# DeltaNet phase of a hybrid block: the order of each head's matmuls given explicitly instead of by a list scheduler

## The chip, the cores and the metric

One core of a Trainium2 chip (trn2). The metric is the device time of one execution in microseconds (us), the median over the runs shown. Engines: PE is the matrix engine (TensorE), PEld its weight loads, DVE the vector engine, ACT the scalar engine, POOL the general engine (GpSimd), SP the engine that issues most DMAs. Each engine works through its own list of instructions in the order of that list; an instruction that is not ready holds up what stands behind it on that engine.

## The reference, cut to what matters

The kernel computes one block of a network: 1024 tokens and 256 context tokens of width 1024; two attention branches over one input projection, gated and merged, then a squared-relu MLP. The change is in the second branch, DeltaNet, with 8 heads of width 128:

```python
def prep(p):
    qkv = silu(depthwise_conv_centred(concatenate([p[3], p[4], p[5]], -1), conv_w))
    q, k, v = split(qkv, 3, -1)
    q = l2_normalize(hd(q)) * DN_HEAD_DIM ** -0.5
    k = l2_normalize(hd(k))
...
def gated_delta_rule(q, k, v, g, beta, s0):          # once forward, once backward
    a_mat = where(strict, einsum('bhnid,bhnjd->bhnij', kb, kc) * decay, 0.0)
    t_mat = triangular_solve(eye + a_mat, eye)        # inverse within a chunk
    ...
    def step(state, xs):
        v_new = u_i - einsum('bhid,bhde->bhie', w_i, state)
        o_i = einsum('bhid,bhde->bhie', q_i, state) + einsum('bhij,bhje->bhie', qk_i, v_new)
        state = state * g_i + einsum('bhid,bhie->bhde', k_i, v_new)
        return state, o_i
...
out_x = rms_norm(ox_f + flip(ox_b), norm_g) * silu(zx)
```

## The kernel before, in words

The DeltaNet phase (`dn_phase`) lies at about 187 to 1340 us of the span. Ahead of it are the modulation of the inputs and small projections; behind it are the attention heads, the merge and the MLP, which the change does not touch but for one call.

A head goes through these parts. **Projections** (`dn_proj` for v, k and q, `dn_gate` for z): each is 48 matmuls of 128x512, two groups of 512 tokens by 8 slices by 3 products (the operands are split in a high and a low part, lines 164 to 166). k, q and v then go through a convolution of 7 taps on DVE (L440; the first tap on ACT, then 6 DVE instructions for each of the two token groups) and Silu on ACT. Further projections that the attention branch needs later are "fills"; they depend on nothing in the heads. **Preparation** (`dn_prep`): sums of squares of k and q for the norms, decay matrices by matmuls (L467, L470), k by k and q by k products (L520, L528), out of which `cm` (the matrix to be inverted, one 128x128 block for each of 10 chunks and both directions) and `pm` come. The 32x32 blocks on the diagonal of `cm` are written to DRAM and read back so that 80 blocks lie in partitions (104 of them with a gap), then inverted by 48 instructions in a row on DVE: a copy (L540), 15 pairs L565 and L566, 4 pairs L573 and L575, 4 pairs L579 and L582, a copy (L545). The inverses go to DRAM again as `xd` and `yd` (L550, L551). **Doubling** (`dn_double`): 7 loads for each direction bring them back into `cm` and `tt` (L596, L599), then 100 matmuls of 32x32 and 40 of 64x64 (both directions together) put the 128x128 inverse together. These are fp32, and an fp32 matmul counts as two passes on PE in the profile. **Tokens** (`dn_pre`): transposes of v and k. **Recurrence** (`dn_chain`): 10 steps for each of two directions; in a step a state matmul (L676), `xs` on DVE (L678), a `cm` matmul (L680), `ws` on ACT (L683), a k matmul (L688), the new state on DVE (L691, L693), and beside it the output (L698 to L707). Then the norm of the output `oacc` on DVE and ACT (to L719), and 8 transposes with the gate (L723, L725).

While the recurrence of head h runs, head h+1 is prepared and v of h+1, k and q of h+2, z of h+1 and fills are projected. In `dn_phase` these are written one after the other; a list scheduler with ranks (0 first: recurrence, doubling, evictions; then preparation and inverse, rank 1; convolution, rank 2) decides where each instruction stands in its engine's list.

The tiles `z32`, `z64`, `tt`, `oacc` have one buffer, `cm` and `pm` four, that is two heads.

Of the kernel before, what the change touches and what calls it, by code (L numbers as in the profile page):

```python
# [35 lines left out]
ORD = 'vkqffz'  # L36
GAP = 8
SPLIT = 508
W1 = (2, 4)
# [14 lines left out]
class K:  # L54
    def __init__(self, tc, ins, out, ctx):
        self.tc, self.nc, self.i, self.out, self.ctx = tc, tc.nc, ins, out, ctx
        self.ranks = None
        self.weng = tc.nc.vector

# [94 lines left out]
    def gemm_cols(self, w, u, toks, evac, cs=slice(0, P), pool=None):  # L154

        nc = self.nc
        rh, rl = u
        for t0, n in toks:
            ps = (pool or self.pg).tile([P, 512], F32, name="pc" if pool else "pg")
            o = ps[:, :n]  # L160
            for k in range(KT):
                hi, lo = w[k][0][:, cs], w[k][1][:, cs]
                a, b = rh[:, k, t0:t0 + n], rl[:, k, t0:t0 + n]
                nc.tensor.matmul(o, lhsT=hi, rhs=a, start=k == 0, stop=False)  # L164
                nc.tensor.matmul(o, lhsT=hi, rhs=b, start=False, stop=False)  # L165
                nc.tensor.matmul(o, lhsT=lo, rhs=a, start=False, stop=k == KT - 1)  # L166
            with self.rank(R_E):
                evac(o, t0, n)
# [246 lines left out]
    def dn_proj(self, h, nm, res):  # L415
# [13 lines left out]
        self.gemm_cols(w, (self.uh, self.ul), TOKS_X, lambda ps, t0, n: nc.scalar.copy(out=raw[:, XO + t0:XO + t0 + n], in_=ps))  # L429
# [13 lines left out]
        res[nm] = acc  # L443

# [5 lines left out]
    def dn_gate(self, h, res):  # L450
        nc, i = self.nc, self.i
        u = (self.uh, self.ul)
        w = self.weight(i["w_in"][0, :, O_DNZ + h * P:O_DNZ + (h + 1) * P])
        sz = self.dw.tile([P, SEQ], F32, name="sz", bufs=1)
        self.gemm_cols(w, u, TOKS_X, lambda ps, t0, n: nc.scalar.activation(out=sz[:, t0:t0 + n], in_=ps, func=AF.Silu))
        res["z"] = sz

    def dn_decay(self, d, h, c0, n, masked):
# [4 lines left out]
        for part, (g, nm) in enumerate(((self.gh[d], "ugh"), (self.gl[d], "ugl"))):  # L463
# [3 lines left out]
            nc.tensor.matmul(pd[:, :n], lhsT=self.r_gt if d == 0 else self.r_lt, rhs=ug[:, :n], start=part == 0,  # L467
                             stop=part == 1 and not masked)
        if masked:
            nc.tensor.matmul(pd[:, :n], lhsT=self.r_id, rhs=self.r_neg[d].unsqueeze(1).to_broadcast((P, n, P)), start=False, stop=True)  # L470
# [4 lines left out]
    def dn_prep(self, h, r):  # L475
# [4 lines left out]
        groups = ((0, 4), (4, 4), (8, 2))  # L480
        ss = ds.tile([P, NT + NX], F32, name="ss")
        ssk, ssq = ss[:, 0:NT], ss[:, NT:]
        for c0, n in groups:
            pt = self.pt.tile([P, 4, P], F32, name="pt")
            for c in range(n):
                nc.tensor.transpose(out=pt[:, c, :], in_=self.ck(kT, c0 + c), identity=self.ident)
            for c in range(n):
                sq = ds.tile([P, P], F32, name="sq", bufs=1)
                nc.scalar.activation(out=sq, in_=pt[:, c], func=AF.Square, accum_out=ssk[:, c0 + c:c0 + c + 1])
        for c0, n in ((0, 4), (4, 4)):  # L490
            pt = self.pt.tile([P, 4, P], F32, name="pt")
            for c in range(n):
                nc.tensor.transpose(out=pt[:, c, :], in_=ch(qT, c0 + c), identity=self.ident)
            for c in range(n):
                sq = ds.tile([P, P], F32, name="sq", bufs=1)
                nc.scalar.activation(out=sq, in_=pt[:, c], func=AF.Square, accum_out=ssq[:, c0 + c:c0 + c + 1])
        nc.vector.tensor_scalar(out=ss, in0=ss, scalar1=RMS_EPS, scalar2=None, op0=ALU.add)
# [18 lines left out]
        for c0, n in ((0, NC0), (NC0, 4), (NC0 + 4, 4)):  # L516
            dec = [self.dn_decay(d, h, c0, n, c0 > 0) for d in range(2)]
            pk = self.pt.tile([P, 4, P], F32, name="pt")
            for c in range(n):
                nc.tensor.matmul(pk[:, c], lhsT=self.ck(kT, c0 + c), rhs=self.ck(kT, c0 + c), start=True, stop=True)  # L520
            for c in range(n):
                for d in range(2):
                    nc.vector.scalar_tensor_tensor(out=cm[d][:, c0 + c], in0=pk[:, c], scalar=nb2[d][:, c0 + c:c0 + c + 1],
                                                   in1=dec[d][:, c], op0=ALU.mult, op1=ALU.mult)
            if c0:
                pk = self.pt.tile([P, 4, P], F32, name="pt")
                for c in range(n):
                    nc.tensor.matmul(pk[:, c], lhsT=self.ck(kT, c0 + c), rhs=ch(qT, c0 + c - NC0), start=True, stop=True)  # L528
                for d in range(2):
                    nc.vector.tensor_tensor(out=pm[d][:, c0 - NC0:c0 - NC0 + n], in0=pk, in1=dec[d], op=ALU.mult)  # L530

# [52 lines left out]
    def dn_double(self, h, r):  # L584
# [3 lines left out]
        tt = []  # L588
        for d in range(2):
            t = dw.tile([P, NT, 64], F32, name="tt", bufs=BK[0])  # L590
            for b, (lo, hi) in (((0, (32, 128)), (1, (64, 128)), (2, (96, 128))) if d else ((1, (0, 32)), (2, (0, 64)), (3, (0, 96)))):
                nc.gpsimd.memset(cm[d][32 * b:32 * b + 32, :, lo:hi], 0.0)
            nc.gpsimd.memset(t[96:128, :, 0:32] if d else t[0:32, :, 32:64], 0.0)
            for b in range(4):
                s = slice(32 * b, 32 * b + 32)
                nc.sync.dma_start(out=cm[d][s, :, s], in_=(yd if d else xd)[d, b].rearrange("c j i -> j c i"))  # L596
                if b != (0 if d else 3):
                    o = 32 * (b % 2)
                    nc.sync.dma_start(out=t[s, :, o:o + 32], in_=(xd if d else yd)[d, b].rearrange("c j i -> j c i"))  # L599
            tt.append(t)  # L600

        for d in range(2):
            c_, t_ = cm[d], tt[d]
            pairs = ((3, 2), (1, 0)) if d else ((0, 1), (2, 3))
            sl = lambda b: slice(32 * b, 32 * b + 32)
            co = lambda b: slice(32 * (b % 2), 32 * (b % 2) + 32)
            pz = self.po.tile([P, NT, 32], F32, name="po")
            z = dw.tile([P, NT, 32], F32, name="z32", bufs=1)
            for a, b in pairs:
                for c in range(NT):  # L610
                    nc.tensor.matmul(pz[sl(b), c], lhsT=c_[sl(a), c, sl(b)], rhs=t_[sl(a), c, co(a)], start=True, stop=True)
                nc.vector.tensor_copy(out=z[sl(b)], in_=pz[sl(b)])
            py = self.po.tile([P, NT, 32], F32, name="po")
            a, b = pairs[0]
            for c in range(NT):
                nc.tensor.matmul(py[sl(b), c], lhsT=c_[sl(b), c, sl(b)], rhs=z[sl(b), c], start=True, stop=True)
            nc.scalar.copy(out=t_[sl(b), :, co(a)], in_=py[sl(b)])
            px = self.po.tile([P, NT, 32], F32, name="po")
            for a, b in pairs:
                for c in range(NT):  # L620
                    nc.tensor.matmul(px[sl(a), c], lhsT=z[sl(b), c], rhs=c_[sl(b), c, sl(b)], start=True, stop=True)
                nc.scalar.copy(out=c_[sl(a), :, sl(b)], in_=px[sl(a)])
            A, B = (slice(64, 128), slice(0, 64)) if d else (slice(0, 64), slice(64, 128))
            z6 = dw.tile([P, NT, 64], F32, name="z64", bufs=1)
            for q in range(2):
                pz = self.po.tile([P, 5, 64], F32, name="po")
                for c in range(5):
                    nc.tensor.matmul(pz[B, c], lhsT=c_[A, 5 * q + c, B], rhs=t_[A, 5 * q + c, :], start=True, stop=True)
                nc.vector.tensor_copy(out=z6[B, 5 * q:5 * q + 5], in_=pz[B])
            for q in range(2):  # L630
                px = self.po.tile([P, 5, 64], F32, name="po")
                for c in range(5):
                    nc.tensor.matmul(px[A, c], lhsT=z6[B, 5 * q + c], rhs=c_[B, 5 * q + c, B], start=True, stop=True)
                nc.scalar.copy(out=c_[A, 5 * q:5 * q + 5, B], in_=px[A])

    def dn_pre(self, h, r):

        nc, dw, ds = self.nc, self.dw, self.ds
        kT, vT = r["k"], r["v"]
        ch = lambda a, c: a[:, c * P:(c + 1) * P]  # L640

        vtok = dw.tile([P, NT, P], F32, name="vtok", bufs=1)
        for c0, n in ((0, 4), (4, 4), (8, 2)):
            pt = self.pt.tile([P, 4, P], F32, name="pt")
            for c in range(n):
                nc.tensor.transpose(out=pt[:, c, :], in_=self.ck(vT, c0 + c), identity=self.ident)
            for c in range(n):
                nc.scalar.activation(out=vtok[:, c0 + c], in_=pt[:, c], func=AF.Copy, scale=r["sk"][:, c0 + c:c0 + c + 1])
        ktok = dw.tile([P, NT, P], F32, name="ktok", bufs=1)
        for c0, n in ((0, 4), (4, 4), (8, 2)):  # L650
            pt = self.pt.tile([P, 4, P], F32, name="pt")
            for c in range(n):
                nc.tensor.transpose(out=pt[:, c, :], in_=self.ck(kT, c0 + c), identity=self.ident)
# [944 lines left out]
```

## Time and profile before

| | |
|---|---|
| median of 3 runs (3024.41, 3024.48, 3035.09) | 3024.48 us |
| the profiled execution's own time | 3038.64 us |
| its span in the profile | 3036.9 us |
| PE busy | 2828.2 us, 93% |
| DVE busy | 2008.3 us, 66% |
| ACT busy | 1333.1 us, 44% |
| POOL busy | 656.6 us, 22% |

How to read the views: a line of the timeline has the start and length of an instruction or a run of alike ones in us, the engine, the line of the kernel, the operation, output<-inputs (tile names), the tile, the type, the count, and in brackets the idle time just before with what ended it. Matmuls are pipelined, so that the step from one start to the next is what one costs, not the length shown. A line of the windows view has start:end and length, then busy us (instructions) of PE, PEld, DVE, ACT and POOL, the granted clock of PE as a share of 2.4 GHz, the DMA share and GB/s.

### The profile page before, as it was taken

How to read it: one execution, taken by the hardware profiler on the slowest of the kernel's cores; microseconds unless marked ns; L12 is line 12 of the kernel's file. 1: busy time of each engine (PE TensorE's matmuls, PEld its weight loads, DVE VectorE, ACT ScalarE, POOL GpSimd, SP SyncE). 2: the span in 40 equal slices, each digit the busy share in tenths (PEclk: the TensorE clock that was granted, in tenths of full speed). 3: DMA queues.
4: the chain of work that ended last, by engine and by line, in shares of the span. 5: the costliest groups of instructions: out<-in, count | busy, mean ns of one | idle time of the engine just before them, and what ended most of it. 6: DMA issues, size and time to landing. Idle time of an engine off the chain costs nothing. (4 is left out here: it accounts for less than half of the span.)

```text
span 3036.9 us, 44469 instructions
## 1 busy us (share of the span) xinstructions
PE 2828.2 (93%) x15928; PEld 2273.6 (75%) x15928; DVE 2008.3 (66%) x3675; ACT 1333.1 (44%) x3269; POOL 656.6 (22%) x756
## 2 busy tenths in 40 slices
PE   7998989899898999989999999899999999989998
PEld 4886768677686777868887778677777677768887
DVE  4768497794967767247777778664486776544435
ACT  4655244444443544326655556564465422322210
POOL 1234223532423241021111110101001643100000
PEclk9999799998998999789999999999999999999999
DMA  7631211211212122173433332416564544453321
GB/s 253 190 110 43 52 48 34 67 53 41 70 33 66 34 63 67 37 186 81 105 93 93 91 88 66 91 39 198 158 220 131 164 143 120 137 194 104 104 63 63
DMA packets 340973, 303.09 MB, mean 100 GB/s; under 512 B 87892, under 2 KB 287700, under 8 KB 339728
## 3 DMA queue, kind: packets, MB, share of 16 engines
q1 hardware_dynamic: 318864, 252.14, 28.5%
q10 hardware_dynamic: 18304, 37.41, 4.8%
q0 software_dynamic: 3584, 10.71, 1.0%
q8 instruction: 125, 2.05, 0.3%
q14 instruction: 96, 0.79, 0.1%
HBM read 212.08 MB, written 66.06 MB: 92 GB/s over the span
## 5 line engine op out<-in xcount | busy, mean ns | idle before, releaser
L150 POOL TENSOR_TENSOR wlo<-wraw,whi 128x256 fp32r<-128x256 f32 x312 | 320.7, 1033 | 1219.5 <-ACT whi L149 987.3
L164 PE MATMUL pg<-uh,whi 128*128 128x512 f32 x1152 | 481.7, 418 | 6.6 <-ACT whi L149 3.2
L166 PE MATMUL pg<-uh,wlo 128*128 128x512 f32 x1152 | 481.3, 418 | 6.1 <-POOL wlo L150 5.8
L165 PE MATMUL pg<-ul,whi 128*128 128x512 f32 x1152 | 481.4, 418 | 0.0
L149 ACT CAST whi<-wraw 128x256 fp32r<-128x256 f32 (+1 forms) x568 | 241.0, 430 | 322.9 <-PE pg L165 102.9
L166 PEld LDWEIGHTS pg<-uh,wlo 128*128 128x128 f32 x1152 | 224.6, 195 | 49.9 <-POOL wlo L150 11.1
L164 PEld LDWEIGHTS pg<-uh,whi 128*128 128x128 f32 x1152 | 224.9, 195 | 47.0 <-ACT whi L149 4.8
L165 PEld LDWEIGHTS pg<-ul,whi 128*128 128x128 f32 x1152 | 224.8, 195 | 39.6
L1370 PE MATMUL pa<-B,A 128*128 128x512 f32 x768 | 220.6, 395 | 13.6 <-ACT B L1318 5.0
L1370 PE MATMUL pg<-B,A 128*128 128x512 f32 x768 | 219.5, 393 | 0.0
L150 DVE TENSOR_TENSOR wlo<-wraw,whi 128x256 fp32r<-128x256 f32 (+1 forms) x256 | 136.6, 542 | 120.8 <-ACT whi L149 119.1
L888 DVE TENSOR_REDUCE mp<-sx 128x1 f32<-128x1024 f32 x128 | 155.7, 1218 | 49.8 <-PE sx L878 49.4
L1370 PEld LDWEIGHTS pa<-B,A 128*128 128x128 f32 x768 | 145.9, 190 | 46.9 <-ACT B L1318 5.4
L1370 PEld LDWEIGHTS pg<-B,A 128*128 128x128 f32 x768 | 146.2, 190 | 30.7
L893 ACT ACTIVATE p<-sx,mx 128x1024 f32<-128x1024 f32 x128 | 143.2, 1118 | 53.2 <-DVE mx L889 41.9
L916 PEld LDWEIGHTS pat<-V,aT 128*128 128x128 f32 x1280 | 151.0, 193 | 14.6 <-ACT aT L914 12.1
L916 PE MATMUL pat<-V,aT 128*128 128x128 f32 x1280 | 158.8, 279 | 0.0
L913 PE MATMUL pat<-ident,p 128*128 128x128 f32 x640 | 119.6, 285 | 8.0 <-ACT oh L917 5.0
L1386 DVE TENSOR_TENSOR acc<-pa,acc 128x512 f32<-128x512 f32 x32 | 22.1, 690 | 157.0 <-PE pa L1370 157.0
L1318 ACT CAST A<-araw 128x1024 fp32r<-128x1024 f32 x32 | 33.6, 1052 | 209.7 <-PE pg L1370 171.8
L913 PEld LDWEIGHTS pat<-ident,p 128*128 128x128 f32 x640 | 74.6, 142 | 56.2 <-ACT aT L914 21.3
L877 PE MATMUL sx<-K,Q 128*128 128x512 f32 x256 | 109.5, 428 | 2.9 <-DMA wraw<-in_w_in_dram 2.0
(457 smaller groups left out, 6701.8 us busy)
## 6 DMA issues: line engine op xcount, KB each, us to landing
wraw<-in_w_in_dram SPq DMA_DIRECT2D x288, 128.0 KB
wraw<-in_w_in_dram SPq DMA_DIRECT2D x64, 256.0 KB
uraw<-in_w_mlp_dram SPq DMA_DIRECT2D x32, 512.0 KB
braw<-in_w_mlp_dram SPq DMA_DIRECT2D x32, 512.0 KB
araw<-ff_d SPq DMA_DIRECT2D x32, 512.0 KB
ff_d<-ue SPq DMA_DIRECT2D x52, 256.0 KB
adraw<-in_w_ada_dram SPq DMA_DIRECT2D x32, 320.0 KB
wa<-in_w_ada_dram SPq DMA_DIRECT2D x8, 1024.0 KB
```

The source lines that it names most:

```text
L149: nc.scalar.copy(out=hi, in_=raw)
L150: self.weng.tensor_tensor(out=lo, in0=raw, in1=hi.bitcast(F32), op=ALU.subtract)
L164: nc.tensor.matmul(o, lhsT=hi, rhs=a, start=k == 0, stop=False)
L165: nc.tensor.matmul(o, lhsT=hi, rhs=b, start=False, stop=False)
L166: nc.tensor.matmul(o, lhsT=lo, rhs=a, start=False, stop=k == KT - 1)
L877: nc.tensor.matmul(ps, lhsT=Q[m][:, qs], rhs=Kh[m][:, ks], start=True, stop=False)
L888: nc.vector.tensor_reduce(out=mp[:, m, 0:1], in_=px[m], axis=AX.X, op=ALU.max)
L893: nc.scalar.activation(out=p[:, CTX:], in_=px[m], func=AF.Exp, bias=mx[:, m:m + 1], accum_out=sp[:, 0, m:m + 1])
L913: nc.tensor.transpose(out=pt[:, c], in_=a[:, (c0 + c) * P:(c0 + c + 1) * P], identity=self.ident)
L916: nc.tensor.matmul(po, lhsT=aT[:, c], rhs=r["v"][:, c], start=c == 0, stop=c == NT - 1)
L1318: nc.scalar.copy(out=z[:, 0], in_=x)
L1370: mm = lambda x, y, **kw: nc.tensor.matmul(ps[c], lhsT=a[:, x, k], rhs=bt[:, y, s], **kw)
```

## The change: the matmuls of a head in a given order

Each matmul and transpose of the phase now goes through `mm` or `tp`, and from the first recurrence on each depends on the one before it, which waits for nothing but fixes PE's order (`pe`, `pinned`). Projections become generators that give one matmul at a time. Between the three parts of a recurrence step ("a" the state matmuls of both directions, "b" the `cm` matmuls, "c" the k and output matmuls) stand 5, 6 and 4 projection matmuls; the next head's preparation comes piece by piece behind parts a and c. Behind the recurrence come the output's transposes after 36 projection matmuls, the tokens from 44 on in five pieces 8 apart, and the next head's doubling in 8 pieces, 8 projection matmuls apart, with 60 left before the first. Both directions are doubled before the next recurrence starts (before, the second direction's doubling stood among the recurrence of the first), and the loads for the second direction are issued after the third piece of the first. z of head h is projected in the round of head h instead of h-1, the number of fills in a round is a table, and the last fills of the attention branch's values move behind the loop. The sums of squares are made in another way: one Square on ACT over the whole tile, then 18 matmuls with 2 columns against ones, where there were 18 transposes and 18 Squares with an accumulator.

```diff
+NFILL = (2, 2, 2, 1, 2, 1, 3, 3)
+GAPS = (5, 6, 4)
+FIN, PRE, PRS, DBL, DBS = 36, 44, 8, 60, 8
...
+    def pe(self, x):
+
+        if self.pinned is not None:
+            if self.pinned:
+                self.tc.add_manual_dep(x.ins, self.pinned, mybir.DependencyInfo(
+                    mybir.DependencyClass.NoSync, mybir.DependencyReason.DATA), reason="given order")
+            self.pinned = x.ins.name
+        return x
+
+    def mm(self, out, lhsT, rhs, start=True, stop=True):
+        return self.pe(self.nc.tensor.matmul(out, lhsT=lhsT, rhs=rhs, start=start, stop=stop))
...
+        if nm != "v":
+            with self.rank(R_PREP):
+                nc.scalar.activation(out=raw[:, 0:acc.shape[1]], in_=acc, func=AF.Square)
+            res["s" + nm] = raw
+
+    def dn_sums(self, nm, r):
...
+        for c in range(n):
+            self.mm(ps[:, c], raw[:, c * P:(c + 1) * P] if nm == "q" else self.ck(raw, c), self.ones)
...
+        self.pinned = ""
         for h in range(H):
...
+            big = self.round(h, proj)
+            left = NBIG[h]
...
+            prep = ranked(self.dn_prep(h + 1, R[h + 1]), R_PREP) if h + 1 < H else iter(())
+            for step, part in self.dn_chain(h, R[h]):
+                take(GAPS["abc".index(part)])
+                if part != "b":
+                    next(prep, 0)
+            all_of(prep)
+
+            rest = [(FIN, lambda: self.dn_finish(h, R[h]))]
             if h + 1 < H:
...
+                pre = ranked(self.dn_pre(h + 1, R[h + 1]), R_PREP)
+                rest += [(PRE + PRS * j, lambda: next(pre)) for j in range(5)]
+                rest += [(max(left - DBL + DBS * j, FIN + 1), x) for j, x in enumerate(self.dn_double(h + 1, R[h + 1]))]
...
+    def round(self, h, proj):
+
+        yield from proj(h + 1, "v")
+        yield from proj(h, "z")
+        n = NFILL[h]
+        yield from self.fill(n // 2)
+        yield from proj(h + 2, "k", "q")
+        yield from self.fill(n - n // 2)
+        if h == H - 1:
+            yield from self.fill_head()
```

Two places show what the lists become. On PE before, in the middle of a round (the doubling of head 2, first direction), the first doubling matmuls (`po<-tt,cm`, fp32) stand among preparation products of the next head (`pt<-kT`, `pt<-qT,kT`) and few projections (`pg`):

```order
L611 MATMUL po<-tt,cm 32x32 x10
L520 MATMUL pt<-kT 128x128 x2
L528 MATMUL pt<-qT,kT 128x128
L616 MATMUL po<-z_5944,cm 32x32 x10
L528 MATMUL pt<-qT,kT 128x128 x3
L621 MATMUL po<-cm,z_5944 32x32 x10
L164 MATMUL pg<-uh,whi 128x512
L165 MATMUL pg<-ul,whi 128x512
L166 MATMUL pg<-uh,wlo 128x512
L611 MATMUL po<-tt,cm 32x32 x10
```

On PE now, in the same doubling (every matmul has the line of the helper, L74):

```order
L74 MATMUL pg<-uh,wlo 128x512
L74 MATMUL po<-tt,cm 32x32 x20
L74 MATMUL pg<-uh,whi 128x512
L74 MATMUL pg<-ul,whi 128x512
L74 MATMUL pg<-uh,wlo 128x512
L74 MATMUL pg<-uh,whi 128x512
L74 MATMUL pg<-ul,whi 128x512
L74 MATMUL pg<-uh,wlo 128x512
L74 MATMUL pg<-uh,whi 128x512
L74 MATMUL pg<-ul,whi 128x512
L74 MATMUL po<-z_5383,cm 32x32 x10
L74 MATMUL po<-cm,z_5383 32x32 x20
```

Moved is what stands between two pieces of the doubling: eight projection matmuls, counted out, with no preparation beside them.

On DVE before, the copy that begins an inverse (L540, that of head 3, in the round of head 2) stands among the recurrence's early steps (`xs` L678, the states L693) and the convolution of v:

```order
L693 SCALAR_TENSOR_TENSOR S_6198<-S_6164,edec,pc_6188 128x128
L440 SCALAR_TENSOR_TENSOR vT<-cvraw,taps,vT 128x516
L678 SCALAR_TENSOR_TENSOR xs_6224<-pc_6222,necg,vtok 128x128
L440 SCALAR_TENSOR_TENSOR vT<-cvraw,taps,vT 128x516
L693 SCALAR_TENSOR_TENSOR S_6152<-S_6132,edec,pc_6144 128x128
L440 SCALAR_TENSOR_TENSOR vT<-cvraw,taps,vT 128x516
L678 SCALAR_TENSOR_TENSOR xs_6173<-pc_6171,necg,vtok 128x128
L540 COPY slL<-slY 40x1024
L565 TENSOR_TENSOR slY<-slX,slL 104x2
L707 TENSOR_TENSOR oacc<-po,oacc 128x128
L693 SCALAR_TENSOR_TENSOR S_6181<-S_6152,edec,pc_6171 128x128
L566 TENSOR_REDUCE slX<-slY 104x2
```

On DVE now, at the same inverse, the copy has the line L570, and the last two `xs` of the recurrence (L729, its tenth step) stand ahead of it:

```order
L767 TENSOR_TENSOR oacc<-po,oacc 128x128
L766 SCALAR_TENSOR_TENSOR oacc<-po,edec,oacc 128x128
L767 TENSOR_TENSOR oacc<-po,oacc 128x128
L729 SCALAR_TENSOR_TENSOR xs_6423<-pc_6420,necg,vk_5301 128x128
L729 SCALAR_TENSOR_TENSOR xs_6426<-pc_6421,necg,vk_5301 128x128
L766 SCALAR_TENSOR_TENSOR oacc<-po,edec,oacc 128x128
L570 COPY slL<-slY 40x1024
L767 TENSOR_TENSOR oacc<-po,oacc 128x128
L766 SCALAR_TENSOR_TENSOR oacc<-po,edec,oacc 128x128
L595 TENSOR_TENSOR slY<-slX,slL 104x2
L767 TENSOR_TENSOR oacc<-po,oacc 128x128
L596 TENSOR_REDUCE slX<-slY 104x2
```

The inverse has moved from among the first steps of the recurrence to behind its last. From this copy to the inverse's last copy (L545 before, L575 now) DVE's list holds 48 instructions of the inverse in both kernels; the others between were 13 of the convolution, 47 of the recurrence and 17 of the norm and output, and are now 18, 3 and 17.

## Rows read from the trace of the kernel before

**Rows 1.** Windows view: the heads' stretch of the phase, then two short ones.

```profile
343.20:1231.00 887.80, 816.93 (x5595) 661.38 (x5594) 644.75 (x1423) 392.18 (x1117) 288.08 (x334) 0.92 0.20 52
676.00:684.00 8.00, 8.00 (x35) 6.31 (x34) 7.44 (x11) 1.99 (x7) 5.21 (x2) 1.00 0.16 57
687.00:697.00 10.00, 10.00 (x79) 8.27 (x80) 0.48 (x1) 5.80 (x20) 2.37 (x7) 0.50 0.42 116
```

**Rows 2.** Timeline of PE: first matmuls of three recurrences (heads 0, 2, 7).

```profile
343.18 0.80 PE L680 MATMUL pc<-vtok,cm 128*128 128x128 f32 x2
...
590.05 0.49 PE L680 MATMUL pc<-vtok,cm 128*128 128x128 f32 x2
...
1230.95 0.79 PE L680 MATMUL pc<-vtok,cm 128*128 128x128 f32 x2
```

**Rows 3.** Waits of PE, 343 to 1231 us: total us, times, longest.

```profile
PE po L723 <- DVE oacc L719: 24.5, 6, 11.0
```

**Rows 4.** DVE by line, 343.2 to 1231 us: busy us, mean ns; idle.

```profile
L440 DVE SCALAR_TENSOR_TENSOR kT<-cvraw,taps,kT 128x772 f32<-128x772 f32 (+1 forms) x72 | 64.0, 888 | 0.0
L440 DVE SCALAR_TENSOR_TENSOR qT<-cvraw,taps,qT 128x516 f32<-128x516 f32 (+1 forms) x72 | 54.4, 767 | 0.4
L565 DVE TENSOR_TENSOR slY<-slX,slL 104x2 f32<-104x2 f32 (+14 forms) x105 | 52.6, 501 | 0.8
...
L579 DVE TENSOR_TENSOR slY<-slL,slX 104x256 f32<-104x256 f32 (+3 forms) x28 | 39.5, 1412 | 0.3
...
L573 DVE TENSOR_TENSOR slY<-slX,slL 104x1024 f32<-104x1024 f32 (+3 forms) x28 | 37.1, 1325 | 0.1
...
L566 DVE TENSOR_REDUCE slX<-slY 104x2 f32<-104x2 f32 (+14 forms) x105 | 33.5, 319 | 0.7
...
L575 DVE TENSOR_REDUCE slL<-slY 104x64 f32<-104x1024 f32 (+3 forms) x28 | 22.7, 810 | 0.1
...
L725 DVE SCALAR_TENSOR_TENSOR sz<-po,dng,sz 128x512 f32<-128x512 f32 x14 | 9.8, 738 | 0.0
...
L719 DVE TENSOR_TENSOR oacc<-oacc,soy 128x1024 f32<-128x1024 f32 x7 | 8.5, 1212 | 0.0
```

**Rows 5.** Timeline of DVE: an inverse's first and last copy, another's last.

```profile
615.94 1.11 DVE L540 COPY slL<-slY 40x1024 f32<-40x1024 f32 x1
...
674.60 1.10 DVE L545 COPY slY<-slX 104x1024 f32<-104x1024 f32 x1
...
1205.11 1.43 DVE L545 COPY slY<-slX 104x1024 f32<-104x1024 f32 x1
```

**Rows 6.** Timeline of PE: the doublings' first matmuls after those two last copies.

```profile
686.95 1.24 PE L611 MATMUL po<-tt,cm 32*32 32x32 f32 x20 [2.31 <-DMA tt<-yd]
...
1211.01 0.79 PE L611 MATMUL po<-tt,cm 32*32 32x32 f32 x20 [1.65 <-DMA tt<-yd]
```

**Rows 7.** Timeline of PE: doubling, then the first steps of a recurrence.

```profile
578.29 0.81 PE L611 MATMUL po<-tt,cm 32*32 32x32 f32 x20
579.04 0.71 PE L520 MATMUL pt<-kT 128*128 128x128 f32 x4
...
588.74 1.37 PE L633 MATMUL po<-cm,z 64*64 64x64 f32 x20
...
590.37 0.83 PE L520 MATMUL pt<-kT 128*128 128x128 f32 x6
...
591.04 0.44 PE L688 MATMUL pc<-ws,ktok 128*128 128x128 f32 x2
...
591.99 0.39 PE L676 MATMUL pc<-S,kT 128*128 128x128 f32 x2
...
593.12 0.38 PE L680 MATMUL pc<-xs,cm 128*128 128x128 f32 x2
```

**Rows 8.** Timeline of ACT: a table load and what follows it.

```profile
705.65 1.28 ACT L455 ACT_TABLE_LOAD   x1
706.95 0.60 ACT L455 ACTIVATE sz<-pg 128x512 f32<-128x512 f32 x1
```

More of the change, by code (lines that the diff above doesn't have):

```diff
@@ L163, in gemm_cols @@
                 a, b = rh[:, k, t0:t0 + n], rl[:, k, t0:t0 + n]
[L164 to L168, printed above, removed]
+                for x, y in ((hi, a), (hi, b), (lo, a)):
+                    self.mm(o, x, y, k == 0 and y is a and x is hi, k == KT - 1 and x is lo)
+                    last = x is lo and k == KT - 1
+                    if last:
+                        with self.rank(R_E):
+                            evac(o, t0, n)
+                    yield
+    def gemm_cols(self, *args, **kw):
+        for _ in self.gemm_steps(*args, **kw):
+            pass
     def gemm_rows(self, u, w, t0, cols, evac, pool):
@@ L454, in dn_gate @@
         sz = self.dw.tile([P, SEQ], F32, name="sz", bufs=1)
[L455 removed]
+        yield from self.gemm_steps(w, u, TOKS_X, lambda ps, t0, n: nc.scalar.activation(out=sz[:, t0:t0 + n], in_=ps, func=AF.Silu))
         res["z"] = sz
@@ L479, in dn_prep @@
         ch = lambda a, c: a[:, c * P:(c + 1) * P]
[L480 to L497, printed above, removed]
+        for nm in "kq":
+            self.dn_sums(nm, r)
+            yield
+        ss = r["ss"]
+        ssk = ss[:, 0:NT]
         rr = self.rsqrt(ds, ss, NT + NX, "kq")
@@ L636, in dn_pre @@
-    def dn_pre(self, h, r):
[L638 to L653, printed above, removed]
-            nc.scalar.copy(out=ktok[:, c0:c0 + n], in_=pt[:, :n])
-        r.update(vtok=vtok, ktok=ktok)
+        sl = lambda b: slice(32 * b, 32 * b + 32)
@@ new lines, in dn_chain @@
+            last = step == NT - 1
+            cs = [order[d][step] for d in range(2)]
+            pc = [self.pc.tile([P, 3, P], F32, name=f"pc{d}") for d in range(2)]
+            S0, xs, ws, wp = list(S), [None] * 2, [None] * 2, [None] * 2
+            with self.rank(R_CHAIN):
+                for d, c in enumerate(cs):
+                    if step == 0:
+                        xs[d] = vk[c][0]
+                        continue
+                    self.mm(pc[d][:, 0], self.ck(kT, c), S0[d])
+                    xs[d] = ds.tile([P, P], F32, name=f"xs{d}", bufs=1)
+                    nc.vector.scalar_tensor_tensor(out=xs[d], in0=pc[d][:, 0], scalar=self.necg[:, d, c, h:h + 1], in1=vk[c][0],
+                                                   op0=ALU.mult, op1=ALU.add)
@@ new lines, in dn_chain @@
+            if step:
+                yield step, "a"
+            with self.rank(R_CHAIN):
+                for d, c in enumerate(cs):
+                    self.mm(pc[d][:, 1], cm[d][:, c], xs[d])
+                    if not last:
+                        ws[d] = ds.tile([P, P], F32, name=f"ws{d}", bufs=1)
+                        nc.scalar.activation(out=ws[d], in_=pc[d][:, 1], func=AF.Copy, scale=bdl[d][:, c:c + 1])
+                if cs[0] >= NC0:
+                    for d, c in enumerate(cs):
+                        wp[d] = ds.tile([P, P], F32, name=f"wp{d}", bufs=1)
+                        nc.scalar.activation(out=wp[d], in_=pc[d][:, 1], func=AF.Copy, scale=b2[d][:, c:c + 1])
@@ L709, in dn_chain, with dn_norm @@
+            if last:
+                with self.rank(R_CHAIN):
+                    self.dn_norm(r, oacc)
+            yield step, "c"
+    def dn_norm(self, r, oacc):
+        nc, ds, rq = self.nc, self.ds, r["rq"]
         so = ds.tile([P, NX], F32, name="so")
@@ L1527, in dn_phase, with all_of @@
     def dn_phase(self):
-        tc = self.tc
         R = [{} for _ in range(H + 2)]
+        def all_of(x):
+            for _ in x:
+                pass
         def proj(h, *names):
@@ L1559, in dn_phase, with ranked @@
-        self.ranks_off()
+                    yield from (self.dn_gate(h, R[h]) if nm == "z" else self.dn_proj(h, nm, R[h]))
+        def ranked(gen, cls):
+            while True:
+                with self.rank(cls):
+                    if next(gen, self) is self:
+                        return
+                yield
+        all_of(proj(0, "k", "q"))
+        all_of(ranked(self.dn_prep(0, R[0]), R_PREP))
+        all_of(proj(0, "v"))
+        all_of(proj(1, "k", "q"))
+        all_of(ranked(self.dn_pre(0, R[0]), R_PREP))
```

273 lines of the change are left out of this document (148 added, 125 removed).

## The prediction, as it was made before the changed kernel ran

> **What bounds the kernel now.** I read the windows first. In the heads' stretch, 343.2 to 1231.0, PE is busy 816.9 of 887.8 us and DVE 644.8, at a mean granted clock of 0.92 [rows 1]. PE is thus the engine to ask about, but it is no solid wall: the clock is below 1 and some waits stay. Next come the starts of the recurrences [rows 2]: from the first (343.18) to the eighth (1230.95) there are seven periods, 887.8 us in all, 126.8 us a head. Third the waits of PE: the largest is that of the output's transposes for the normed `oacc`, 24.5 us in 6 heads, the longest 11.0 [rows 3]. Last the timeline around an inverse: DVE's copy that begins head 3's starts 615.94, the copy that ends it 674.60, over at 675.70 [rows 5]; PE's first doubling matmul that needs the loaded blocks comes at 686.95 after an idle 2.31 [rows 6]. Inverse, loads, doubling, recurrence: a chain runs through each head, and before, the inverse began 25.9 us after the recurrence of the head in front (590.05 [rows 2] to 615.94 [rows 5]).
>
> **The change part by part.** Lists are in order on each engine, so the order rows tell what stands before what, and the trace tells what it costs. The copy that begins the inverse now stands behind the `xs` of the recurrence's tenth step, and PE's doubling behind counted projections. That closes a loop from one recurrence to the next: recurrence up to its tenth state matmul (PE), that `xs` (DVE), DVE's list up to the inverse's last copy, loads, doubling (PE), next recurrence. Its five pieces, for a middle head:
>
> First, doubling to recurrence on PE: 60 projection matmuls, 200 passes of 32x32, 80 of 64x64. A warm projection matmul is 0.23 us (8.00 us hold 35 records, two of them cut at the edges, at clock 1.00 [rows 1]); a 32x32 pass is (579.04 - 578.29)/20 = 0.0375, a 64x64 pass (590.05 - 588.74)/20 = 0.0655 [rows 2, 7]. 13.8 + 7.5 + 5.2 = 26.5 us.
>
> Second, recurrence to its tenth state matmul on PE: by the order 130 projection matmuls, 99 fp32 matmuls of 128 columns (recurrence and preparation), 16 decay matmuls and 18 of the new sums. 130 x 0.23 = 29.9; 198 passes at (591.04 - 590.37)/6 = 0.112 [rows 7] are 22.2; the decay, 12 of 512 columns and 4 of 256, priced as projections by columns, 3.2. A matmul with 2 columns is nowhere in before; nothing would be its lower bound, a 128-column pass (36 x 0.112 = 4.0) its upper; I take the smallest matmul there is, 36 x 0.0375 = 1.4. Together 56.7 us. Before, the inverse did not wait for this.
>
> Third, state matmul to `xs` done: the matmul of a step at 591.99, the next `cm` matmul, which needs `xs`, at 593.12: 1.1 us [rows 7].
>
> Fourth, DVE from the inverse's first to its last copy. The inverse by the means of [rows 4]: 15 x 0.501 + 15 x 0.319 + 4 x (1.325 + 0.810 + 1.412), and 0.81 for each of the last four reductions, which have the size of L575's: 7.5 + 4.8 + 5.3 + 3.2 + 5.6 + 3.2 = 29.6, and 2.4 for the two copies [rows 5]. The 18 convolution instructions, 12 of k and 6 of q, are 12 x 0.888 + 6 x 0.767 = 15.3. The 17 of the norm and output: 1.2 (L719), two at 0.74 (L725), 14 small ones at some 0.3 (estimate, from L566's): 6.9. Three of the recurrence, 0.9. Sum 55. Such a sum counts overlap twice: before's own list between [rows 5]'s copies, priced in the same way, is 66, and took 59.8 (615.94 to 675.70), a share of 0.91. So 50 us; 55, no overlap at all, is the upper bound, and 48, a share of 0.87, the lower one: none of before's seven lists, priced so, comes out below that. In two rounds the list has two convolution instructions fewer (-1.6 each), in the last none (-14).
>
> Fifth, last copy to first doubling matmul: 675.70 to 686.95 is 11.3, 1206.54 to 1211.01 is 4.5 [rows 5, 6]. I take 8, nearly the middle; the loads themselves are the same.
>
> The pieces make 26.5 + 56.7 + 1.1 + 50 + 8 = 142.3 us. Between the tenth state matmul and the doubling, PE has only 98 projection matmuls and 28 transposes, 22.5 + 56 passes x 0.112 = 28.8 us, while DVE and the loads take 59: PE stands still some 30 us a head. A part of that falls on the output's transposes, which again wait for `oacc`, and the rest directly on the doubling; behind that wait all else on PE is queued, since the order is given. After a wait the clock falls: after the 2.31 us of [rows 6] the ten microseconds from 687 were granted 0.50, the 1.2 GHz level [rows 1], and hold what five would at 2.4 GHz. So +5, with nothing as the lower bound: 147.3 a head.
>
> Edits with no term of their own: the new sums take 18 transposes (4.0 us of PE) and 18 small Squares of ACT away for the 1.4 above, and the counts already have them; as PE now waits, what is saved outside the loop buys nothing. z and the values' fills move to places with slack, their DMAs with them. Prologue and tail: the inverse of head 0 is no earlier, its doubling now stands bare (a few us more), and after the last recurrence there is less left; I take the two together as nothing, 8 either way.
>
> ACT: `ws` and the evictions share its list with Silu, Square and Exp, whose tables have to be loaded; the order has 16 table loads more in the phase, two a head. A load is 1.28 us and the next instruction starts 0.02 us behind it [rows 8]: 16 x 1.28 = 20.5 us more on an engine that is busy 392.2 of 887.8 [rows 1]. Only a load in front of a `ws` or a doubling's eviction reaches the loop; I give it nothing, up to 16 x 1.28 as the other end, which the range holds. The Trainium skill, "ScalarE: Activation LUTs", section "What ACT_TABLE_LOAD costs", has the same 1283 ns load and a drain of about 1380 ns besides, 2.66 us a switch. By it the 16 would be 42.6 us, twice the sum's other end; [rows 8] show no such gap behind the load, so I go by the row.
>
> Sum: 7 x 147.3 - 17 (the shorter lists) = 1014 us between first and last recurrence, against 887.8: +126. The profiled execution took 3038.6, 14 us above the median of 3024.5; 3038.6 + 126 = 3165, on the median's scale some 3150 us.
>
> **The rivals.** Faster: the blocks are there when PE comes. Then PE's 26.5 + 56.7 + 28.8 = 112 us is the period, and the time 3024 + 7 x (112 - 126.8) = 2920. List and loads would have to fit in 29 us; with the inverse alone (32 x 0.91 = 29) and the shortest load of 4.5 the period is 118 and the time about 2960. For it speaks that PE's order has no waste and DVE has 27% idle in the stretch; against it the 35 other instructions in the list. It decides as soon as list and loads are below (126.8 + 2.4) - 84.3 = 45 us with no half clock (2.4 is 17/7), against my 58.
>
> Low bounds together: list 48, loads 4.5, no half clock: 136.8 a head, 7 x 136.8 - 17 - 888 = +53, 3078; with the recurrence's 56.7 a few us shorter too, down to no change, 3030.
>
> The recurrence itself stretched: `xs` stands behind convolutions of 0.7 to 0.9 us on DVE, `ws` behind evictions and table loads on ACT, and PE, whose order is given, waits at each of some 20 places instead of taking other work. 0.4 us at each is 8 a head, +56: 3200 and more, with loads of 11.3 about 3235.
>
> That the order isn't what is said is excluded by the order rows.
>
> **How the numbers follow.** The loop as summed, 3060 to 3200: 0.63, predicted 3150. Faster: 0.14. The low bounds, 3009 to 3060: 0.12, of which 0.07 within 0.5% of before (15 us, about what a measurement of this kernel can tell from no change). The stretched recurrence, above 3200: 0.11. Faster by over 0.5% 0.14, within 0.07, slower 0.79. The range from 3020 to 3240 leaves out the faster case, a little below 3040 and the end of the last.
>
> **What would show it.** Recurrence starts some 147 us apart; the inverse's first copy 57 to 58 us after the recurrence's first matmul; about 50 us to its last copy; PE idle before the output's transposes (some 10 to 15 us, released by the normed `oacc`) and before the first doubling matmul (15 to 20 us, released by the loads of `tt` or `cm`), and a granted clock of 0.50 for some 10 us behind that. It would be wrong if the list took under 40 us, if `oacc` and loads show no wait of PE, or if waits within the recurrence exceed those two.

## The result, and the profile after

The changed kernel takes 3251.5 us (median of 4 runs, 3240.3 to 3261.8) against 3029.5 us (4 runs) for the one before: ratio 1.073, 95% interval 1.0685 to 1.0778. It is slower, as forecast, and by 222 us where 126 were forecast; 3251 lies 11 us above the range.

The profiled execution after is the lowest of its four (3240.3), the one before was the highest (3038.6), so the two traces are 202 us apart. In the windows view of the trace after, the first line is the heads' stretch, first to last recurrence, as in [rows 1]; then come the first recurrence, and for a middle round DVE's part, the doubling and the recurrence:

```profile
321.30:1415.90 1094.60, 844.36 (x6017) 714.31 (x6017) 661.98 (x1492) 406.23 (x972) 296.36 (x369) 0.85 0.17 43
321.30:398.90 77.60, 74.68 (x524) 66.16 (x523) 41.83 (x117) 33.18 (x75) 26.08 (x38) 0.87 0.13 29
554.90:612.60 57.70, 30.12 (x141) 24.18 (x140) 48.52 (x89) 18.23 (x51) 16.67 (x11) 0.79 0.18 52
612.60:648.00 35.40, 33.09 (x340) 26.20 (x341) 8.43 (x14) 10.23 (x20) 4.36 (x7) 0.82 0.18 40
648.00:708.90 60.90, 59.92 (x382) 53.32 (x381) 39.30 (x113) 31.45 (x71) 26.46 (x38) 1.00 0.17 42
```

The heads' stretch grew from 887.8 to 1094.6, by 207 us. The first recurrence starts 22 us earlier than before (321.3 against 343.2), and what follows the last one is 17 us longer (3238.5 - 1415.9 against 3036.9 - 1231.0): 207 - 22 + 17 = 202. Projections moved along: by count of the trace 203 fewer stand ahead of the first recurrence, 84 more between first and last, 119 more behind.

The waits of PE in that stretch (total us, times, longest), to hold against [rows 3]:

```profile
PE po L74 <- DMA tt<-yd: 170.9, 12, 32.9
PE po L77 <- DVE oacc L786: 54.2, 7, 8.0
PE po L74 <- ACT cm L665: 7.1, 14, 0.5
```

225 us over seven rounds are the doubling's wait for its blocks and the output's transposes' wait for `oacc`; [rows 3] had 24.5 of the second, and of the first, in the same stretch of the kernel before, there were 4.0:

```profile
PE po L611 <- DMA tt<-yd: 4.0, 2, 2.3
```

The loop can be followed on three engines. On PE, the recurrence starts, its last state matmuls (those of the tenth step) come, the output's transposes and the next doubling wait, and the next recurrence starts (timeline, head 2's recurrence to head 3's):

```profile
648.01 0.60 PE L74 MATMUL pc<-vk,cm 128*128 128x128 f32 x4
...
651.22 2.29 PE L74 MATMUL pt<-ones,cvraw 128*128 128x2 f32 x20
653.37 0.69 PE L74 MATMUL pc<-S,kT 128*128 128x128 f32 x4
...
708.61 0.61 PE L74 MATMUL pc<-S,kT 128*128 128x128 f32 x4
...
729.98 1.97 PE L77 MATMUL po<-ident,oacc 128*128 128x128 f32 x8 [7.57 <-DVE oacc L786]
...
766.43 1.24 PE L74 MATMUL po<-tt,cm 32*32 32x32 f32 x20 [19.07 <-DMA tt<-yd]
...
801.69 0.61 PE L74 MATMUL pc<-vk,cm 128*128 128x128 f32 x4
```

On DVE, in the same round, the first copy of the inverse and the last:

```profile
712.70 0.35 DVE L766 SCALAR_TENSOR_TENSOR oacc<-po,edec,oacc 128x128 f32<-128x128 f32 x1 [3.06 <-PE po L74]
713.09 1.11 DVE L570 COPY slL<-slY 40x1024 f32<-40x1024 f32 x1
...
759.91 1.03 DVE L575 COPY slY<-slX 104x1024 f32<-104x1024 f32 x1
```

DVE stood still 3.06 us ahead of an `oacc` instruction that the inverse's first copy is queued behind, and began the copy 65.1 us after the recurrence's start, where before it was 25.9 ([rows 2, 5]). From there the chain is closed: 47.9 us to the end of the last copy (760.94), 5.5 to the doubling, 35.3 to the next recurrence.

### The profile page after: what moved, and what is told of

Read it like the earlier page. It is cut to its first block, busy times and chain, and to the rows that moved or that the text cites. A ratio compares the mean times of both kernels' runs of the same rounds, so it can differ in the third digit from the quotient of the medians.

```text
span 3238.5 us, 44455 instructions
## 1 busy us (share of the span) xinstructions
PE 2807.6 (87%) x16072; PEld 2296.8 (71%) x16072; DVE 1993.9 (62%) x3683; ACT 1322.5 (41%) x3029; POOL 631.5 (19%) x756
## 5 line engine op out<-in xcount | busy, mean ns | idle before, releaser
L169 POOL TENSOR_TENSOR wlo<-wraw,whi 128x256 fp32r<-128x256 f32 x312 | 292.1, 939 | 1294.2 <-ACT whi L168 1039.1
L74 PE MATMUL pg<-uh,whi 128*128 128x512 f32 x1152 | 493.9, 429 | 5.4 <-ACT whi L168 4.6
L74 PE MATMUL pg<-ul,whi 128*128 128x512 f32 x1152 | 485.1, 421 | 0.0
L74 PE MATMUL pg<-uh,wlo 128*128 128x512 f32 x1152 | 479.8, 417 | 4.1 <-POOL wlo L169 4.0
L74 PEld LDWEIGHTS pg<-uh,wlo 128*128 128x128 f32 x1152 | 227.8, 198 | 53.6 <-POOL wlo L169 6.9
L74 PEld LDWEIGHTS pg<-uh,whi 128*128 128x128 f32 x1152 | 228.6, 198 | 47.8 <-ACT whi L168 5.8
L74 PEld LDWEIGHTS pg<-ul,whi 128*128 128x128 f32 x1152 | 229.6, 199 | 37.5
L74 PE MATMUL po<-tt,cm 32*32 32x32 f32 (+1 forms) x960 | 61.4, 227 | 219.8 <-DMA tt<-yd 212.4
L74 PEld LDWEIGHTS po<-tt,cm 32*32 32x32 f32 (+1 forms) x960 | 55.0, 141 | 236.8 <-issue 182.1
L987 PEld LDWEIGHTS pat<-V,aT 128*128 128x128 f32 x1280 | 149.7, 192 | 13.5 <-ACT aT L985 11.2
```

Of the source, the lines that this page charges most:

```text
L74: return self.pe(self.nc.tensor.matmul(out, lhsT=lhsT, rhs=rhs, start=start, stop=stop))
L169: self.weng.tensor_tensor(out=lo, in0=raw, in1=hi.bitcast(F32), op=ALU.subtract)
L987: nc.tensor.matmul(po, lhsT=aT[:, c], rhs=r["v"][:, c], start=c == 0, stop=c == NT - 1)
```

## The experiments

Ratios are to the kernel before on the same chip, with 95% intervals; the changed kernel stands at 1.073. A period, or round, runs from the start of one recurrence to the start of the next; it is 154 us for a middle head of the changed kernel.

**e1, free order.** The dependency from matmul to matmul is left out:

```diff
-        self.pinned = ""
         for h in range(H):
```

> The changed kernel with the matmuls written in the same places but without the dependency from each to the next, so that the list scheduler orders PE. Loop theory (what costs is that the inverse starts behind the recurrence, that DVE's list follows, and that the doubling waits at its counted place): by the order rows the inverse's first copy moves up to the 3rd to 7th step again, so the wait before the doubling shrinks and most of the 222 us come back: 3030 to 3100. Rival (the cost is in the other edits: both directions doubled before the recurrence, new sums, more table loads, fills moved): still 3180 or more.

1.0209 (1.0175 to 1.0243). Without the fixed order 5.2 of the 7.3 per cent are gone. The inverse of head 3 begins 23 us after the recurrence in front of it (652.5 against 629.4), the wait of PE for the blocks is not among the three largest any more (below), the doubling to recurrence takes 12 to 30 us. PE waits, e1:

```profile
PE po L77 <- DVE oacc L786: 48.8, 7, 18.6
PE pg L74 <- POOL wlo L169: 22.3, 7, 11.7
PE pt L74 <- DVE cm L550: 7.8, 3, 4.1
```

So the order is the larger part, and the other edits cost 2.1% when the order is left to the scheduler.

**e2, late doubling.**

```diff
-FIN, PRE, PRS, DBL, DBS = 36, 44, 8, 60, 8
+FIN, PRE, PRS, DBL, DBS = 36, 44, 8, 24, 3
```

> Doubling with 24 projection matmuls left instead of 60 and 3 between its pieces instead of 8. Loop theory: PE waits for the loads anyway, so the 36 projection matmuls that move ahead of the doubling fill the wait, and a head gets shorter by 36 x 0.23 = 8.3 us, 7 x 8.3 = 58 us: about 3190 (3165 if half-clock stretches go with them; waits within the doubling for its copies can eat half of it). Rival (PE's work sets the period, not the loop): no change, 3250.

1.069 (1.0663 to 1.0717): no gain clear of noise. It is not that PE's work sets the period, as the rival had it: the wait for `tt` fell from 170.9 to 120.4 us, and PE still stands there. The doubling still took 35.9 us, with 36 projection matmuls fewer in it, and the windows view of that stretch says why:

```profile
775.70:811.60 35.90, 33.38 (x305) 26.65 (x306) 3.90 (x8) 5.55 (x14) 2.89 (x5) 0.50 0.13 25
```

The whole doubling was granted 0.50, the 1.2 GHz level, where the changed kernel's was granted 0.82; so it was in five of the seven rounds, and 0.60 in the other two. What fewer matmuls saved, the slower clock took. DVE's list, besides, took 50 to 52 us instead of 47 to 48 in all rounds but the last.

**e3, early preparation.**

```diff
-                if part != "b":
-                    next(prep, 0)
+                next(prep, 0)
```

> A piece of the next head's preparation after every part of the recurrence, not after two of three. The order shows the inverse's first copy behind 14 xs instead of 18, two steps earlier. Loop theory: 2 steps x 6 us + 3 us for the output that stood ahead of it, less about 4 us for 14 more instructions in the list: 10 to 12 us a head, about 3170. Rival (PE's work sets the period): no change, 3250; rival (the recurrence gets stretched, since preparation crowds it): slower.

1.0614 (1.0578 to 1.0649), half of what was expected. The inverse begins 9.4 us ahead of the last state matmul instead of 4.1 behind, 13.5 us won. 8 to 9 go in the recurrence, now 70 us long at a clock of 0.90, and in most rounds 3 to 9 in the doubling; the wait for `oacc` grew from 54.2 to 93.9 us.

**e4, convolutions behind the inverse.** Each DVE instruction of the convolutions of k and q depends (order only) on the inverse's last copy:

```diff
+                    if nm != "v" and self.inv is not None:
+                        self.tc.add_manual_dep(x.ins, self.inv, ...)
...
+            self.inv = x.ins.name if h else None
```

> The convolutions of k and q ordered on DVE behind the inverse's last copy. DVE's list from first to last copy then has no convolution, as that of the last head has, which took 35.7 us against 48. Loop theory: 12.5 us a head less in six rounds, about 3175; some of it goes if the doubling's copies then stand behind convolutions. Rival (the list's length is covered): no change.

1.0494 (1.047 to 1.0518). The two copies of one round in the timeline of DVE:

```profile
548.43 1.14 DVE L574 COPY slL<-slY 40x1024 f32<-40x1024 f32 x1
...
584.25 1.03 DVE L579 COPY slY<-slX 104x1024 f32<-104x1024 f32 x1
```

36.9 us instead of 48: 11.3 a round won, 3.9 given back in the doubling (39.3 instead of 35.4), where PE now waits 30.1 us in all for the `z` copies that stand behind convolutions. 147 us a round. The list's length is on the path, as the loop has it.

**e5, a warm PE ahead of the doubling.** 90 extra matmuls ahead of the first piece:

```diff
+                        for _ in range(90):
+                            self.mm(wt.rearrange("p a b -> p (a b)"), self.uh[:, 0, 0:P], self.uh[:, 0, 0:3 * P])
```

> The changed kernel with 90 extra matmuls of 384 columns (their result is not used) ahead of each doubling's first piece, 90 x 0.17 = 15.6 us, less than the 19 us and more that PE waits there. Clock theory (a good part of what the prediction missed is PE at 0.50 behind the wait): the doubling's first 6 us run at the full clock, 3 to 6 us a head less, ratio to before down from 1.073 to between 1.06 and 1.065. Rival (the doubling is slow through its own short waits and small passes, whatever stands ahead): no change; a rival on the other side: the extra matmuls come out late and add up to 15 us a head.

1.0719 (1.0682 to 1.0755): no change. The idle ahead of the doubling is 3.7 us instead of 19.0 (in four of seven rounds; 16.7 in two), and the stretch ahead of it was granted 0.97, yet the doubling took 37.7 us at 0.75 (windows, ahead of it and in it):

```profile
590.00:613.10 23.10, 19.37 (x110) 18.41 (x109) 17.76 (x22) 5.78 (x12) 4.44 (x4) 0.97 0.19 51
613.10:650.80 37.70, 35.41 (x340) 28.25 (x341) 8.44 (x14) 10.24 (x20) 4.35 (x7) 0.75 0.17 38
```

This does not test what it was meant to test. The extra matmuls end before the blocks come, so an idle of 3.7 us is left directly ahead of the doubling, more than the 2.31 us from which the prediction took its half clock ([rows 1, 6]), and behind it the doubling runs at 0.50 for 15 us. What a doubling does with no idle ahead is seen in e6 and e8.

**e6, no inverse.**

```diff
-            self.inverse32(NB)
+            if h == 0:
+                self.inverse32(NB)
```

> Leaves out the 46 instructions of the inverse on DVE for heads 1 to 7 (the two copies stay; the blocks are then the identity, and the output with them not the reference's). Loop theory: DVE's list shrinks from 48 to about 20 us, the wait before the doubling nearly goes, and the period falls from 154 to 125 to 130 us, ratio about 1.01 to 1.02; what stays above 112 is the clock in the doubling and the wait for the normed output. Rival (PE's given order and its clock set the period): the period stays above 145, ratio above 1.05.

0.9941 (0.9918 to 0.9964), below even the loop theory's figure, since DVE's list from copy to copy took 2.3 to 3.6 us and not the 20 expected. The period is 120 to 124 us in the middle rounds, and PE's wait for the blocks is

```profile
PE po L74 <- DMA tt<-yd: 1.9, 1, 1.9
```

With DVE's list out of the loop the same given order, recurrence (61 us) and doubling (32 to 37) run some 30 us a round faster. That is the price of the loop, and it decides against the rival that order and clock alone set the period. The kernel before without its inverse was not run; the nearest to it is e12, where a shorter list gains nothing in the kernel before.

**e7, the new sums alone, in the kernel before.**

```diff
+            nc.scalar.activation(out=raw[:, 0:acc.shape[1]], in_=acc, func=AF.Square)
...
+                nc.tensor.matmul(ps[:, c], lhsT=..., rhs=self.ones, start=True, stop=True)
```

> The kernel before with the new sums of squares alone (one Square over the tile and 18 matmuls with 2 columns). If the sums are worth what PE saves, 2.6 us a head where PE is busy, 7 x 2.6 = 18 us: ratio 0.994. If they are worth nothing (PE waits elsewhere) 1.00. If they are part of the 2.1% that the free order still costs: above 1.005.

1.009 (1.0055 to 1.0124): a cost, not a saving. PE saves nothing (see below), and `cvraw`, which has two buffers, is now held until the sums have read it: POOL, which clears the edges of the next one, waits 34.2 us in all for these matmuls. That this wait is what costs the 0.9% was not tested.

**e8, e3 + e4 + e5.**

> The edits of e3, e4 and e5 together on the changed kernel. Loop theory: the convolutions off the list (11 us, of which e4 gave 4 back), the inverse up to two steps earlier (13 us, of which e3 gave back 8 in a longer recurrence) and a warm doubling (3 to 6): a period of 135 to 140, ratio 1.02 to 1.035, still slower than before. Rival (each only moves the wait to the output's transposes): no better than e4, 1.05.

1.0825 (1.079 to 1.086), slower than the changed kernel. The blocks are there early, but PE comes to the doubling 20 to 34 us after the inverse's last copy, where the loads took some 5: it waits 103.6 us in all for `oacc`, and the extra matmuls of e5, which had lain in a wait, come behind that and cost their 15 us.

For the clock e6 and e8 decide what e5 left open, since in them PE works right up to the doubling. The first 6 us of a doubling, in the changed kernel, e5, e6 and e8 (windows; 15 us for e5):

```profile
766.43:772.00 5.57, 4.96 (x46) 4.30 (x47) 0.98 (x2) 0.00 (x0) 0.00 (x0) 0.50 0.40 63
613.10:628.50 15.40, 14.19 (x126) 11.37 (x126) 0.98 (x2) 3.37 (x7) 1.46 (x2) 0.50 0.21 39
545.04:551.04 6.00, 4.96 (x89) 4.07 (x88) 3.37 (x5) 4.68 (x11) 2.20 (x3) 1.00 0.19 45
629.15:635.15 6.00, 4.97 (x89) 4.07 (x88) 0.98 (x2) 1.24 (x3) 0.72 (x1) 1.00 0.02 4
```

In the changed kernel and in e5 an idle of 3.6 us or more lies directly ahead of every one of the seven doublings, and all run at 0.50 from their start or within 2 us of it. All seven of e8 and five of e6 have no such idle and start at 1.00; the two of e6 that start at 0.50 come 2 us behind a wait of 9.8 us for `oacc`. So the half clock at the start does come with the idle ahead. It is not the only one: further on each of these doublings has stretches at 0.50 all the same, in four of e8 one of some 10 us from the third or fourth us on. On the mean of seven rounds the doubling takes 34.6 us in e6 and 34.9 in e8, against 37.1 in the changed kernel.

**e9, e8 without the extra matmuls, output's transposes later.**

```diff
-FIN, PRE, PRS, DBL, DBS = 36, 44, 8, 60, 8
+FIN, PRE, PRS, DBL, DBS = 78, 36, 8, 60, 8
```

> e8 without the extra matmuls, and with the output's transposes after 78 projection matmuls instead of 36, the tokens from 36 on. Loop theory: PE no longer meets the normed output early, comes to the doubling in time, and the period is what the loop makes it: 69 (recurrence as in e3) - 9 + 37 + 5 + 36 to 40 = 138 to 142, ratio 1.025 to 1.035. Rival (recurrence and doubling stretch by as much as the inverse comes earlier, as in e3): 1.05 as e4.

1.0359 (1.0306 to 1.0412), just past the end of the expected range: periods of 140 to 147 us in the middle rounds, waits for the blocks 39.9 and for `oacc` 32.3 us. The lowest ratio of the kernels with the given order that compute everything, though e10's interval overlaps its own.

**e10, e4 with the same line.**

> e4 with the output's transposes after 78 projection matmuls and the tokens from 36 on. Loop theory: the wait for the normed output, 8 us a head, was inside the wait before the doubling, so that moving it changes nothing: as e4, 1.049. Rival (each wait costs for itself): 8 us a head less, 1.03.

1.0405 (1.0357 to 1.0453), between the two expectations. The wait for `oacc` is gone, that for the blocks rose from 94.0 to 131.5: the 8 us moved into the other wait. The gain is in the two rounds with fewer fills (140 instead of 147 us) and in the last (137). In these three the 78 matmuls ahead of the output's transposes leave few for the doubling: it holds 296 matmuls instead of some 359 and takes 29 to 33 us instead of 41 to 42, at a clock of 0.54.

**e11, free order and the old sums.** e1 with the 18 transposes and 18 Squares back.

> e1 (free order) with the old sums, 18 transposes and 18 Squares with accumulators. If the new sums carry their 0.9% of e7 here too, the ratio falls from e1's 1.021 to about 1.012, and the rest lies with the doubling of both directions ahead of the recurrence and the moved projections. If not, it stays at 1.02.

1.0093 (1.0059 to 1.0126). The new sums cost 1.2% here, as in e7 they cost 0.9%.

**e12, e4's edit in the kernel before.**

> The kernel before with the convolutions of k and q ordered on DVE behind the inverse's last copy. By the order rows the inverse then stands behind 15 xs with nothing between its instructions: about 32 us instead of 57 to 74, but begun some 20 us later, and the convolutions begin later too. In before PE is busy 92% and waits little for the blocks, so: within 1% of before, faster only if the 24 us of waits for the normed output go.

0.9997 (0.9969 to 1.0025): no change. The list shrinks to 35 to 38 us in most rounds and begins 18 to 52 us later in all but the first; before, with 4.0 us of waits for the blocks, has next to nothing there to win.

**e13 and e14, what lowers the clock in the doubling.** Extra matmuls of 384 columns, four at the wait in the second piece (e13), or 16 a direction among its 32x32 matmuls (e14):

```diff
+                    if (a, b) == pairs[1]:
+                        self.spare(4)
```

> The changed kernel with 4 extra matmuls of 384 columns (result unused), 0.7 us, where PE waits 0.5 us for ACT's copy of cm in the middle of the doubling's second piece, in both directions. If that short idle is what lowers the clock behind it: no half-clock stretch there, doubling to recurrence 36 us down to 31 to 33, ratio about 1.06. If the run of small passes ahead of it does: the clock falls all the same, doubling as long as before or 1.4 us longer, 1.073 to 1.078.

> The changed kernel with 16 extra matmuls of 384 columns a direction among the 32x32 matmuls of the doubling's second piece, 32 x 0.17 = 5.4 us a head more on PE. If the run of small passes lowers the clock, it now holds: the stretch behind the second piece is granted 1.00, which gives back 3 to 4 us in each direction, doubling to recurrence 34 to 36 us, 1.065 to 1.073. If neither that nor the short wait matters: 5 us a head more, doubling 41 us, ratio about 1.085.

e13 1.0705 (1.0646 to 1.0764), e14 1.1045 (1.0987 to 1.1103). Neither keeps the clock up through the doubling. In e13 the doubling takes 36 to 41 us in six of seven rounds. The half-clock stretch behind the second piece is gone where the clock was up at that piece, as the theory of the short idle had it, but others come instead: in two rounds one behind the second direction's first piece, and in four one of 10 us in the next recurrence, which then takes 65 to 66 us instead of 61. The windows view of e13, behind the second piece, then those two:

```profile
624.00:636.00 12.00, 11.88 (x134) 9.40 (x129) 5.61 (x9) 4.73 (x9) 1.10 (x2) 1.00 0.16 33
637.50:641.00 3.50, 3.50 (x14) 2.29 (x14) 0.29 (x1) 0.60 (x1) 0.00 (x0) 0.53 0.11 39
658.00:668.00 10.00, 10.00 (x37) 8.89 (x36) 3.46 (x23) 0.74 (x2) 0.71 (x4) 0.50 0.09 26
```

The last of these comes with no idle of PE shown since 0.58 us at 636.46. In e14 the doubling takes 49 to 55 us, more than either expectation, and the clock falls in the midst of the second direction's second piece, with no idle of PE shown since 0.58 us at 659.27 (timeline of PE):

```profile
667.62 0.44 PE L74 MATMUL pc<-uh 128*128 128x384 f32 x1
667.99 0.37 PE L74 MATMUL po<-cm,z 32*32 32x32 f32 x6
668.29 0.69 PE L74 MATMUL pc<-uh 128*128 128x384 f32 x1
...
670.60 0.63 PE L74 MATMUL pg<-uh,wlo 128*128 128x512 f32 x1
671.03 0.63 PE L74 MATMUL pg<-uh,whi 128*128 128x512 f32 x1
```

0.43 us from one projection to the next, where 0.23 is the step at 1.00. So the idle ahead goes with the half clock at the doubling's start (e6, e8), but neither the short wait nor the lone run of 32x32 passes explains the later stretches by itself. What does stays open.

## Why the prediction was wrong in size

**The loop.** Right: the inverse behind the recurrence's end, DVE's list, the doubling at its counted place, PE's stall of 32 us a head (30 forecast), in the middle round 7.6 for `oacc` (10 to 15 forecast) and 19.1 for the blocks (15 to 20). e6 takes the list out and the period falls by some 32 us, e4 shortens it and the period follows. e1 frees the order and most of the loss is gone.

**The size.** The terms of the sum, for a middle head (612.6 to 766.4, 153.8 us against 147.3 forecast) and over the seven rounds:

| piece | forecast | middle head | seven rounds, measured less forecast |
|---|---|---|---|
| doubling to recurrence | 31.5 | 35.4 | +39 |
| recurrence to tenth state matmul | 56.7 | 60.9 | +49 |
| to the inverse's first copy | 1.1 | 4.1 | +21 |
| DVE's list | 50 | 47.9 | -10 |
| loads | 8 | 5.5 | -18 |

Sum +81, and 126 + 81 = 207. The mechanism of the loop held, but three terms of its sum were too small, by 109 us together; that the list and the loads came out 28 below hid a part of it.

The recurrence: the new sums. I priced a 2-column pass at 0.0375 us, nearest to the smallest matmul of [rows 7]. In the rows above, 20 of them take 653.37 - 651.22 = 2.15 us, 0.107 each, as much as a pass of 128 columns: 36 are 3.9 us, the upper bound that I named. The same row tells why e7 finds no saving: the transposes took 4.0. Of the other 1.7 us some 1.1 are one stop of PE for ACT's `wp` (0.98 us idle at 693.87). The rest is the change between fp32 and projections: the first projection behind fp32 takes 0.32 instead of 0.23 us at 26 places, 2.2 us, and of that the fp32 passes give 1.8 back, as they took 0.102 and not 0.112 each. In the first round the recurrence takes 77.6 us, since the second direction of head 0's doubling falls into it; the earlier start pays for that (-22), and I had put both at nothing. In one round (from 956.6) a half-clock stretch adds 3.

The inverse's first copy: I took it to follow `xs`. In the order rows an `oacc` instruction (L766) stands between, and it waits for the output matmuls behind 11 more projections: 3.06 us.

The doubling: 5 us were laid to a half clock behind the wait. Full speed would be 26.5; 35.4 x 0.18 = 6.4 us went to the clock and 2.3 to short waits of PE for copies and loads that I had not counted (`tt` 0.70, `cm` 0.51 twice, `z` 0.58). The idle ahead does bring the half clock at the start, as I said (e6, e8), but in this head for some 6 us and not 10, so that it costs 3 us. What the sum lacked are two more stretches of some 3 us at 0.50, one in each direction behind the second piece; they and the short waits are the miss.

Behind the last recurrence I had nothing; 119 projections moved there and that part is 17 us longer.

**The rest.** ACT's table loads: 42 instead of 22 in the heads' stretch, 53.9 against 28.2 us, and PE waited there only 6.9 us for ACT's `wp`, 1 us a head, in the middle head behind such a load (691.15): taking nothing was nearly right. The instruction behind a load starts 0.01 us (median) after it there, and the load 0.02 us after the instruction ahead of it, so no run here shows the drain of about 1.38 us that the Trainium skill, "ScalarE: Activation LUTs", section "What ACT_TABLE_LOAD costs", adds to a load. The stretched recurrence did not come: 60 of its 60.9 us PE was busy, at clock 1.00.

**Left open:** what lowers the clock further on in the doubling and, in e13, in the recurrence, and 0.9% of the other edits (e11), among them the doubling of both directions ahead of the recurrence, the places of z and of the fills.

No version here that computes everything beats the kernel before. e6 shows how far the given order could come with the inverse off the loop, 0.994, and it leaves the inverse out; a deeper pipeline, which would need another set of `cm` and `pm`, was not tried.

## What to carry to other kernels

When an order is fixed on one engine, look for the loop that closes through another engine's list: what stands ahead of the first instruction that the fixed engine will wait for, and how long the list is to the last. Matmuls counted out ahead of a wait cover only what PE needs for them (29 us here against 57 on DVE and in the loads). And an edit that makes one wait shorter is worth its time only until the next: e3, e4 and e10 each gave a third or more back to the wait or the clock behind it.

## What was not expected of the hardware

A matmul with 2 columns costs as much as one with 128 in fp32 on this path: 0.107 us a pass. A doubling with 24 projection matmuls among 280 small passes, behind an idle of 12.8 us, ran at the 1.2 GHz level from end to end though PE was busy 33.4 of its 35.9 us (e2); the changed kernel's, with 60, was granted 0.82 on the mean. Extra matmuls ahead of it that still left 3.7 us of idle did not raise that (e5, 0.75), nor did extra matmuls within it (e13 0.83, e14 0.71 in the rounds shown); without an idle ahead it was 0.90 in the rounds shown of e6 and e8.
